# Up projection by seven block products in its own stage, with the down projection behind it

## The chip, the cores and the metric

The kernel runs on one core of one Trainium2 chip. The metric is device time in microseconds, from runs of the whole program; the profile is one further execution of it, recorded instruction by instruction. TensorE (PE) multiplies, with its weight loads listed apart (PEld); VectorE (DVE), ScalarE (ACT) and GpSimd (POOL) do the elementwise work; SyncE (SP) and POOL issue transfers. SBUF is the on-chip memory of the operands, PSUM that of the accumulators; what is named DRAM here lies off the core.

## The reference

One layer of a decoder trunk over 512 prompt tokens and 8 x 4 sample tokens, all in float32:

```python
x += W_o [ swish(g) * GroupNorm(Retention(q_r, k_r, v_r)) ; SlidingWindowSinkGQA(q_s, k_s, v_s) ]
hn = rmsnorm(x, ffn_norm_w)
up = hn @ w_up                     # 2048 x 11264: gate half g, up half u
gp = concat([conv_buf, g]); gc = conv_b + sum(gp[:, j:j+T] * conv_w[j] for j in range(3))
x += (silu(gc) * u) @ w_down       # 5632 x 2048
```

Outputs are x for both kinds of tokens, the retention states, the key and value windows, and the last two rows of g.

## The kernel before

Tokens lie in the columns: 544 of them, as two halves u of HC = 272 (256 prompt columns and 16 sample columns each). Features lie in the 128 partitions: D = 2048 is 16 tiles, the feed-forward width 5632 is FT = 44. A float32 operand is split in two parts, `hi` (a cast to fp32r on ACT, line 149) and `lo` (the difference on DVE, line 150). A product of two split operands is three matmul passes, lo x hi, hi x lo and hi x hi: `mm3`, lines 167 to 178, first those with a low part (line 173), then the high ones (line 177). Each matmul has 128 x 128 weights, a weight load of its own and 272 moving columns; the two halves u go to two PSUM banks in turn.

`project` (line 180) makes one output tile of 128 features from 2048: 16 x 6 = 96 matmuls. Its weights come in two halves of 1024 rows (512 KB each) through `stage_half`: `wraw` (3 buffers), split into `whi` and `wlo` (3 buffers each). A_hi and A_lo (16 tiles) hold the split input, C the unsplit one.

The order of the stages is: the combined input projection with retention and attention between its projects (lines 812 to 916); the output projection (918 to 992), which for each of 16 output tiles m multiplies the attention half of the input (in B) and the retention half (in A), adds the kept input, squares for the norm (POOL sums the squares, line 978) and writes the normed tile into A (`split_hn`, lines 937 to 940); and the feed-forward (999 on). There `up_group(G)` computes two feature tiles f: project the gate tile, multiply by 1/rms, convolve along the tokens (lines 1025 to 1028), project the up tile, multiply, split into Hh and Hl. `down_group(G - 1)` then multiplies the two tiles of the group before by w_down for all 16 output tiles, 12 matmuls each, and adds each into C on DVE (line 1071). In the last group `emit_y` transposes finished tiles and stores them.

The program's text is not the order of issue: a scheduler of the framework fixes the instruction order on every engine when the program is built, by which instructions it takes to be ready, earlier ones in the text first, and sets the waits. On the chip each engine then goes through its list in order. A buffer of a pool comes free when its last reader has finished; pools that lie in the space of a closed pool wait for the tiles whose space they take.

## Time and profile before

| | |
|---|---|
| median of 3 runs | 2409.63 us (2408.25 to 2410.67) |
| span of the profiled execution | 2409.4 us |
| PE busy | 2390.8 us, 99% |
| PEld busy | 2348.2 us, 97% |
| DVE busy | 1205.1 us, 50% |
| ACT busy | 651.7 us, 27% |
| DMA | 225.85 MB, 94 GB/s |

Of the profiled execution only the span is recorded, which lies 0.2 us under the median of the runs. The page of the profile gives the busy time of each engine, and groups instructions by line. A busy PE is not one at its peak, since matmuls overlap one another; its pace is read from start to start. The chain that ended last follows the work back from the last instruction; "issue" in it is time without a recorded reason. The waits say who waited for whom. The windows give busy times in stretches of the span.

### The profile page before, as it was taken

The page shows a single profiled execution, that of the slowest core. Times are in us where ns is not written, and L with a number is a line of the kernel's source. Part 1 is how long each engine was busy: PE and PEld are TensorE (multiplying, and loading weights), DVE is VectorE, ACT ScalarE, POOL GpSimd, SP SyncE. Part 2 cuts the span into 40 slices and gives each one's busy share as a digit, 9 for nine tenths or more (in the row PEclk, how much of TensorE's full clock was granted, in tenths as well). Part 3 has the DMA queues.
Part 4 walks back from the last instruction along what each step waited for, and adds up shares of the span by engine and source line. Part 5 has one row for each costly group of instructions (what it writes and reads, how often), then busy time and mean ns, then how long its engine had stood idle before and what let it go on. Part 6 is the DMA issues. An engine that isn't in the chain of part 4 may idle for free.

```text
span 2409.4 us, 43062 instructions
## 1 busy us (share of the span) xinstructions
PE 2390.8 (99%) x18743; PEld 2348.2 (97%) x18743; DVE 1205.1 (50%) x2033; ACT 651.7 (27%) x974; POOL 69.9 (3%) x240
## 2 busy tenths in 40 slices
PE   8999999999999999999999999999999999999999
PEld 7999999999999999999999999999999999999998
DVE  5545467765432544455444555444555444555444
ACT  5121235555222322222222222222222222222223
POOL 1000000000011000000000000000000000000000
PEclk8999999999999999999999999999999999999999
DMA  8333342223444332222332332323333323223223
GB/s 273 103 85 97 77 89 67 73 71 93 113 110 106 88 88 88 88 88 88 88 88 88 88 88 88 88 86 90 87 88 89 87 86 88 87 89 89 88 85 106
DMA packets 360269, 225.85 MB, mean 94 GB/s; under 512 B 41937, under 2 KB 331793, under 8 KB 360081
## 3 DMA queue, kind: packets, MB, share of 16 engines
q1 hardware_dynamic: 358576, 217.70, 32.0%
q0 software_dynamic: 1504, 5.41, 0.6%
q8 instruction: 147, 2.41, 0.4%
q14 instruction: 42, 0.34, 0.0%
HBM read 205.48 MB, written 12.86 MB: 91 GB/s over the span
## 4 chain that ended last, share of the span: by engine, by line
PE 97%; DMA 1%; SPq 1%; issue 1%; ACT 0%; DVE 0%; ACTq 0%
PE acc L173 60%; PE acc L177 30%; PE sm L719 1%; PE sm L718 1%; DMA raw<-in_w_o_dram 1%; PE sm L680 1%; PE sm L697 1%; SPq L231 0%; DMA raw<-in_w_in_dram 0%; PE sm L528 0%; PE sm L526 0%; PE sm L491 0%; PE sm L551 0%; PE sm L541 0%; PE sm L1050 0%
## 5 line engine op out<-in xcount | busy, mean ns | idle before, releaser
L173 PE MATMUL acc<-A_lo,whi 128*128 128x272 f32 x4160 | 869.2, 290 | 0.8 <-ACT whi L149 0.6
L173 PE MATMUL acc<-A_hi,wlo 128*128 128x272 f32 x4160 | 864.3, 289 | 0.0
L149 ACT CAST whi<-raw 128x1024 fp32r<-128x1024 f32 x364 | 381.6, 1048 | 1388.5 <-PE acc L177 1351.5
L150 DVE TENSOR_TENSOR wlo<-raw,whi 128x1024 fp32r<-128x1024 f32 x364 | 444.8, 1222 | 462.6 <-ACT whi L149 462.3
L173 PEld LDWEIGHTS acc<-A_lo,whi 128*128 128x128 f32 x4160 | 655.0, 189 | 7.3 <-issue 4.2
L173 PEld LDWEIGHTS acc<-A_hi,wlo 128*128 128x128 f32 x4160 | 652.4, 188 | 1.2
L177 PE MATMUL acc<-A_hi,whi 128*128 128x272 f32 x4160 | 571.3, 289 | 0.0
L177 PEld LDWEIGHTS acc<-A_hi,whi 128*128 128x128 f32 x4160 | 541.9, 189 | 1.2
L1071 DVE TENSOR_TENSOR C<-acc,C 128x544 f32<-128x544 f32 x352 | 250.7, 722 | 134.9 <-PE acc L177 133.1
L173 PE MATMUL acc<-Hl,whi 128*128 128x272 f32 x1408 | 292.3, 289 | 0.0
L173 PE MATMUL acc<-Hh,wlo 128*128 128x272 f32 x1408 | 291.3, 288 | 0.0
L177 PE MATMUL acc<-Hh,whi 128*128 128x272 f32 x1408 | 232.9, 287 | 0.0
L173 PEld LDWEIGHTS acc<-Hh,wlo 128*128 128x128 f32 x1408 | 220.2, 188 | 0.0
L173 PEld LDWEIGHTS acc<-Hl,whi 128*128 128x128 f32 x1408 | 219.5, 188 | 0.2
L177 PEld LDWEIGHTS acc<-Hh,whi 128*128 128x128 f32 x1408 | 198.0, 188 | 0.0
L1031 DVE TENSOR_TENSOR us<-acc,rstd_bc 128x544 f32<-128x544 f32 x44 | 31.9, 725 | 162.7 <-PE acc L177 162.7
L1017 DVE TENSOR_TENSOR gp<-acc,rstd_bc 128x512 f32<-128x512 f32 x44 | 30.4, 692 | 162.6 <-PE acc L177 162.5
L1028 ACT ACTIVATE cv<-cv,cwT 128x560 f32<-128x560 f32 x44 | 33.6, 764 | 136.5 <-DVE cv L1027 136.5
L173 PE MATMUL acc<-B_hi,wlo 128*128 128x272 f32 x256 | 53.3, 289 | 0.0
L173 PE MATMUL acc<-B_lo,whi 128*128 128x272 f32 x256 | 53.1, 288 | 0.0
L1021 POOL COPY co<-gp 128x2 f32<-128x2 f32 x44 | 8.2, 187 | 1372.2 <-DVE gp L1017 1372.2
L978 POOL TENSOR_TENSOR ssq<-ssq,sq 128x544 f32<-128x544 f32 x15 | 26.4, 1762 | 539.5 <-ACT sq L977 539.5
(375 smaller groups left out, 1355.8 us busy)
## 6 DMA issues: line engine op xcount, KB each, us to landing
raw<-in_w_up_dram SPq DMA_DIRECT2D x176, 512.0 KB
raw<-in_w_down_dram SPq DMA_DIRECT2D x88, 512.0 KB
raw<-in_w_in_dram SPq DMA_DIRECT2D x52, 512.0 KB
raw<-in_w_in_dram SPq DMA_DIRECT2D x32, 256.0 KB
raw<-in_w_o_dram SPq DMA_DIRECT2D x32, 256.0 KB
raw<-in_w_o_dram SPq DMA_DIRECT2D x16, 512.0 KB
C<-in_x_prompt_dram SPq DMA_DIRECT2D x8, 512.0 KB
xT_keep<-xk POOLq DMA_DIRECT2D x16, 256.0 KB, 6.1
```

What stands on the lines that cost most here:

```text
L149: act.copy(out=hi, in_=src)
L150: eng.tensor_tensor(out=lo, in0=src, in1=hi.bitcast(F32), op=sub)
L173: pe.matmul(acc[:, u, :HC], lhsT=w, rhs=x[:, u, :], start=(first and i == 0 and w is wh), stop=False)
L177: pe.matmul(acc[:, u, :HC], lhsT=wh, rhs=xh[:, u, :], start=False, stop=(last and i == n - 1))
L680: pe.matmul(po[:, 256 * kv:256 * kv + 256], lhsT=vS[:, n if n == 0 else n - 1 + kb, kv, :], rhs=t[:, kb, :], start=(j == 0), stop=(j == le ...
L697: pe.transpose(out=ptr[:, o:o + 128], in_=s[:, 2 * j + kv, 128 * kb:128 * kb + 128], identity=ident)
L718: pe.matmul(o, lhsT=q_, rhs=kX[kv][:, k0:k0 + 256], start=True, stop=False)
L978: pool.tensor_tensor(out=ssq, in0=ssq, in1=sq, op=add)
L1017: dve.tensor_tensor(out=gp[:, 2:514].rearrange("p (u c) -> p u c", u=2), in0=ag[:, :, 0:256], in1=rstd_bc[:, :, 0:256], op=mult)
L1028: act.activation(out=cva, in_=cva, func=AF.Silu, bias=cb[:, f:f + 1])
L1031: dve.tensor_tensor(out=us, in0=au, in1=rstd_bc, op=mult)
L1071: dve.tensor_tensor(out=C[:, m], in0=acc[:, :, :HC], in1=C[:, m], op=add)
```

## The change

The up projection becomes a stage of its own. For each f, the gate tile f and the up tile f, times two halves of the input features, times two halves of the tokens, are a 2 x 2 by 2 x 2 block product. It is computed with seven products of 1024 x 128 weight blocks and 272 token columns (24 matmuls each) in place of eight. The weight sums are formed on DVE in `up_pair`, the sums of the input blocks once, in `build_x`, in place in C. Partial sums are read out of PSUM by ACT in the middle of accumulations (bank `bx`, and one half of `zy`) and put together on DVE. The product of gate and up part goes to DRAM (`h_keep`), by POOL's queue. The down projection stands behind it in three groups of 16, 12 and 16 tiles f: `fill` loads them back and splits them, `down` accumulates a whole group in PSUM for two output tiles at a time. The output projection goes in two passes over m, first the attention half of its input, then the retention half; the sum x goes to DRAM (`x1_keep`) and comes back into Y for the down stage. C and the weight buffers move to the right side of the memory, so that the up stage's buffers (`ua`, `ub`) can take their place; `ring` takes turns between both.

```diff
-    wp = ctx.enter_context(tc.tile_pool(name="wp", bufs=3))
...
+    cp_ = cst.enter_context(tc.tile_pool(name="cp", bufs=1, side="right"))
+    wp = wst.enter_context(tc.tile_pool(name="wp", bufs=3, side="right"))
...
-    C = main.tile([128, KT, 2, HC], F32, name="C")
+    C = cp_.tile([128, KT, 2, HC], F32, name="C")
...
+    x1_keep = keep.tile([KT, 128, 2, HC], F32, name="x1_keep")
+    h_keep = keep.tile([FT, 128, 2, HC], F32, name="h_keep")
...
-        wo = wst.enter_context(tc.tile_pool(name="wo", bufs=1, reuse_waits="tile"))
+        mid = xst.enter_context(tc.tile_pool(name="mid", bufs=1, reuse_waits="tile"))
...
+        wo = bst.enter_context(tc.tile_pool(name="wo", bufs=1, reuse_waits="tile"))
...
+    def half_project(m, part, xh, xl):
+        hi, lo = stage_half(load_wo(m, part), 0)
+        acc = ps.tile([128, 2, 512], F32, name="acc", tag="acc", bufs=3)
+        for _ in mm3(acc, [(hi[:, k, :], lo[:, k, :], xh[:, k], xl[:, k]) for k in range(8)]):
...
+        return acc[:, :, :HC]
...
+        acc = half_project(m, 0, B_hi, B_lo)
...
+    bst.close()
+    xp = xst.enter_context(tc.tile_pool(name="xp", bufs=1, reuse_waits="tile"))
+    X_hi = xp.tile([128, 3, 8, HC], F32R, name="X_hi")
+    X_lo = xp.tile([128, 3, 8, HC], F32R, name="X_lo")
+    xop = {
+        "b21": (A_hi[:, 0:8, 0], A_lo[:, 0:8, 0]), "t4": (A_hi[:, 0:8, 1], A_lo[:, 0:8, 1]),
+        "b22": (A_hi[:, 8:16, 0], A_lo[:, 8:16, 0]), "t3": (A_hi[:, 8:16, 1], A_lo[:, 8:16, 1]),
+        "b11": (X_hi[:, 0], X_lo[:, 0]), "t1": (X_hi[:, 1], X_lo[:, 1]), "t2": (X_hi[:, 2], X_lo[:, 2]),
...
+    def split_x(name, k, src, sign=1.0):
+        hi, lo = (t[:, k] for t in xop[name])
+        if sign == 1.0:
+            split(hi, lo, src)
+        else:
+            act.activation(out=hi, in_=src, func=AF.Copy, scale=sign)
+            dve.scalar_tensor_tensor(out=lo, in0=src, scalar=sign, in1=hi.bitcast(F32), op0=mult, op1=sub)
...
+    def build_x(k):
+        a, b, c, d = C[:, k, 0], C[:, k, 1], C[:, k + 8, 0], C[:, k + 8, 1]
+        split_x("b11", k, a)
+        dve.tensor_tensor(out=b, in0=d, in1=b, op=sub)
+        split_x("t3", k, b)
+        dve.tensor_tensor(out=b, in0=b, in1=a, op=add)
+        split_x("t2", k, b, -1.0)
+        dve.tensor_tensor(out=a, in0=b, in1=d, op=sub)
+        split_x("t1", k, a)
+        split_x("b22", k, d)
+        dve.tensor_tensor(out=d, in0=b, in1=c, op=sub)
+    for i in range(KT):
+        m = i // 2 + 8 * (i % 2)
+        acc = half_project(m, 1, A_hi[:, 0:8], A_lo[:, 0:8])
+        dve.tensor_tensor(out=C[:, m], in0=acc, in1=C[:, m], op=add)
+        sth(out=x1_keep[m], in_=C[:, m])
+        if i == 0:
             act.activation(out=ssq, in_=C[:, m], func=AF.Square)
         else:
+            sq = tb1.tile([128, 2, HC], F32, name="sq2", tag="sq2", bufs=1)
             act.activation(out=sq, in_=C[:, m], func=AF.Square)
             pool.tensor_tensor(out=ssq, in0=ssq, in1=sq, op=add)
-        if m < 8:
-            split_hn(m)
-        if m == 2:
-            stT, w0, w1, w2, cb = conv_tables()
-    for m in range(8, 16):
-        split_hn(m)
-    up_ops = ((A_hi[:, 8:16], A_lo[:, 8:16]), (A_hi[:, 0:8], A_lo[:, 0:8]))
+        act.activation(out=C[:, m], in_=C[:, m], func=AF.Copy, scale=ffnw[:, m:m + 1])
+        if i % 2 == 1:
+            build_x(i // 2)
+    for k in range(8):
+        split(A_hi[:, k], A_lo[:, k], C[:, k + 8])
...
+    wst.close()
...
+    cst.close()
+    ub = ust2.enter_context(tc.tile_pool(name="ub", bufs=1, side="right", reuse_waits="tile"))
+    def ring(name, shape, dtype, n_a, n_b):
...
+    new_raw = ring("uraw", [128, 8, 128], F32, 2, 3)
+    new_sum = ring("usum", [128, 8, 128], F32, 1, 1)
+    new_hi = ring("uhi", [128, 8, 128], F32R, 2, 1)
+    new_lo = ring("ulo", [128, 8, 128], F32R, 2, 1)
+    new_g = ring("g", [128, 562], F32, 2, 0)
+    new_cv = ring("cv", [128, 562], F32, 1, 1)
+    new_tu = ring("tu", [128, 2, HC], F32, 1, 1)
+    new_us = ring("us", [128, 2, HC], F32, 1, 1)
+    new_p5 = ring("p5", [128, HC], F32, 1, 1)
...
-    ag0 = project(ps, 3, stage(cols_of(w_up[0], 0)), up_ops, between={48: rstd_ffn})
+    rstd_ffn()
...
+    def product(bank, w, x, first, last):
+        hi, lo = new_hi(), new_lo()
+        split(hi, lo, w)
+        xh, xl = xop[x]
+        for k in range(8):
+            pe.matmul(bank, lhsT=hi[:, k], rhs=xl[:, k], start=(first and k == 0), stop=False, skip_group_check=True)
+            pe.matmul(bank, lhsT=lo[:, k], rhs=xh[:, k], start=False, stop=False, skip_group_check=True)
+        for k in range(8):
+            pe.matmul(bank, lhsT=hi[:, k], rhs=xh[:, k], start=False, stop=(k == 7), skip_group_check=True)
+    def up_pair(f):
+        def load(c0, q):
+            raw = new_raw()
+            cols_of(w_up[0], c0)(raw, q)
+            return raw
+        a11, a21, a22, a12 = load(128 * f, 0), load(DFF + 128 * f, 0), load(DFF + 128 * f, 1), load(128 * f, 1)
+        bx = ps.tile([128, 512], F32, name="bx", tag="bx", bufs=2)[:, :HC]
+        zy = ps.tile([128, 2, 512], F32, name="zy", tag="zy", bufs=2)[:, :, :HC]
+        tu, us, p5 = new_tu(), new_us(), new_p5()
+        product(bx, a11, "b11", True, False)
+        act.copy(out=tu[:, 0], in_=bx)
+        s1 = new_sum()
+        dve.tensor_tensor(out=s1, in0=a21, in1=a22, op=add)
+        product(zy[:, 1], s1, "t1", True, False)
+        act.copy(out=p5, in_=zy[:, 1])
+        s2 = new_sum()
+        dve.tensor_tensor(out=s2, in0=s1, in1=a11, op=add)
+        product(bx, s2, "t2", False, False)
+        act.copy(out=tu[:, 1], in_=bx)
+        dve.tensor_tensor(out=s2, in0=s2, in1=a12, op=add)
+        product(zy[:, 1], s2, "b22", False, True)
+        dve.tensor_tensor(out=a21, in0=a21, in1=a11, op=add)
+        product(bx, a21, "t3", False, False)
+        act.copy(out=us[:, 1], in_=bx)
+        product(zy[:, 0], a12, "b21", True, True)
+        g = new_g()
...
+        dve.tensor_tensor(out=gp, in0=zy[:, :, 0:256], in1=tu[:, :, 0:256], op=add)
...
+        dve.tensor_tensor(out=gp, in0=gp, in1=rstd_bc[:, :, 0:256], op=mult)
...
+        cv = new_cv()
+        cva = cv[:, 0:560]
+        act.activation(out=cva, in_=g[:, 2:562], func=AF.Identity, scale=w2[:, f:f + 1], bias=cb[:, f:f + 1])
+        dve.scalar_tensor_tensor(out=cva, in0=g[:, 1:561], scalar=w1[:, f:f + 1], in1=cva, op0=mult, op1=add)
+        dve.scalar_tensor_tensor(out=cva, in0=g[:, 0:560], scalar=w0[:, f:f + 1], in1=cva, op0=mult, op1=add)
+        act.activation(out=cva, in_=cva, func=AF.Silu)
+        product(bx, a22, "t4", False, True)
+        act.copy(out=us[:, 0], in_=bx)
+        dve.tensor_tensor(out=us[:, 1], in0=us[:, 1], in1=p5, op=add)
+        dve.tensor_tensor(out=us, in0=us, in1=rstd_bc, op=mult)
+        dve.scalar_tensor_tensor(out=us[:, :, 0:256], in0=us[:, :, 0:256], scalar=-1.0, in1=halves_of(cv[:, 0:512]), op0=mult, op1=mult)
...
+        sth(out=h_keep[f], in_=us)
+    for f in range(FT):
+        up_pair(f)
+    ust2.close()
+    ust.close()
...
+    places = [(Xf_hi[:, i], Xf_lo[:, i]) for i in range(12)] + [(A_hi[:, i], A_lo[:, i]) for i in (*range(8, 16), *range(8))]
+    groups, at_ = [], 0
+    for n, p0 in ((16, 0), (12, 16), (16, 0)):
+        groups.append((range(at_, at_ + n), places[p0:p0 + n]))
...
+    def fill(group):
+        for f, (hi, lo) in zip(*group):
+            hs = dn.tile([128, 2, HC], F32, name="hs", tag="hs", bufs=2)
+            ld(out=hs, in_=h_keep[f])
+            split(hi, lo, hs)
...
-    def down_group(G, Hh, Hl):
-        for q in range(4):
-            raw = wraw().rearrange("p k c -> p (k c)").rearrange("p (j c) -> p j c", j=2)
-            ld(out=raw, in_=wd[256 * G:256 * G + 256, 512 * q:512 * q + 512].rearrange("(j p) c -> p j c", p=128))
-            hi, lo = (t.rearrange("p k c -> p (k c)").rearrange("p (j c) -> p j c", j=2) for t in whalf())
+    def down(group, mp, last):
+        fs, where = group
+        accs = [ps.tile([128, 2, 512], F32, name="acc", tag="acc", bufs=3) for _ in range(2)]
+        for j in range(len(fs) // 4):
+            f0 = fs[0] + 4 * j
+            raw, hi, lo = (dn.tile([128, 4, 256], d_, name=n_, tag=n_, bufs=b_) for n_, d_, b_ in (("draw", F32, 3), ("dhi", F32R, 2), ("dlo", F32R, 2)))
+            ld(out=raw, in_=wd[128 * f0:128 * f0 + 512, 256 * mp:256 * mp + 256].rearrange("(j p) c -> p j c", p=128))
             split(hi, lo, raw)
-            for i in range(4):
-                m = 4 * q + i
-                acc = ps.tile([128, 2, 512], F32, name="acc", tag="acc", bufs=3)
+            for i in range(2):
                 c = slice(128 * i, 128 * i + 128)
-                for _ in mm3(acc, [(hi[:, j, c], lo[:, j, c], Hh[:, j], Hl[:, j]) for j in range(2)]):
+                for _ in mm3(accs[i], [(hi[:, t, c], lo[:, t, c], *where[4 * j + t]) for t in range(4)], j == 0, 4 * j + 4 == len(fs)):
...
-                dve.tensor_tensor(out=C[:, m], in0=acc[:, :, :HC], in1=C[:, m], op=add)
-                if G == FT // 2 - 1 and m >= YLAG:
-                    emit_y(m - YLAG)
...
+        for i in range(2):
+            m = 2 * mp + i
+            dve.tensor_tensor(out=Y[:, m], in0=accs[i][:, :, :HC], in1=Y[:, m], op=add)
+            if last and m >= YLAG:
...
+    for m in range(KT):
+        ld(out=Y[:, m], in_=x1_keep[m])
+    fill(groups[0])
+    down(groups[0], 0, False)
+    fill(groups[1])
...
+    for mp in range(1, 8):
+        down(groups[0], mp, False)
+    fill(groups[2])
+    for mp in range(8):
+        down(groups[1], mp, False)
+    for mp in range(8):
+        down(groups[2], mp, True)
...
```

## Rows read from the trace of the kernel before

In rows of a timeline the columns are start and duration in us, engine, line, operation, output <- inputs, partitions x elements, count, and in brackets the idle time before with what ended it.

**Rows 1.** The page, parts 1 and 5: engine shares, and one group of weight loads

```profile
PE 2390.8 (99%) x18743; PEld 2348.2 (97%) x18743; DVE 1205.1 (50%) x2033; ACT 651.7 (27%) x974; POOL 69.9 (3%) x240
...
L173 PEld LDWEIGHTS acc<-A_lo,whi 128*128 128x128 f32 x4160 | 655.0, 189 | 7.3 <-issue 4.2
```

**Rows 2.** Windows: length; busy (count) by engine; clock, DMA share, GB/s

```profile
0.00:57.50 57.50, 45.91 (x317) 43.45 (x317) 29.41 (x54) 33.31 (x55) 10.98 (x25) 0.88 0.93 285
...
640.00:650.00 10.00, 8.56 (x60) 7.97 (x59) 3.81 (x6) 2.09 (x2) 0.67 (x1) 0.83 0.78 166
...
800.00:812.00 12.00, 12.00 (x95) 11.84 (x94) 10.35 (x15) 9.82 (x13) 2.98 (x5) 1.00 0.22 62
...
1036.00:1108.40 72.40, 72.40 (x579) 72.40 (x578) 35.34 (x46) 15.43 (x17) 1.17 (x8) 1.00 0.29 88
```

**Rows 3.** Chain that ended last in order of time (start, us, what), one loop period

```profile
1506.22 4.03 PE acc L173 x32
...
1578.59 4.03 PE acc L173 x32
```

**Rows 4.** Waits (waited for: us in total, times, longest): weight splits on ACT

```profile
ACT whi L149 <- PE acc L177: 1351.5, 326, 8.2
```

**Rows 5.** Timeline of PE in the attention, line 680: first pair and what follows

```profile
406.83 0.40 PE L680 MATMUL sm<-pl,vS 128*128 128x256 f32 x2
...
407.77 2.17 PE L177 MATMUL acc<-A_hi,whi 128*128 128x272 f32 x16
```

**Rows 6.** Groups by line and form on DVE: busy us, mean ns

```profile
L150 DVE TENSOR_TENSOR wlo<-raw,whi 128x1024 fp32r<-128x1024 f32 x364 | 444.8, 1222 | 462.6 <-ACT whi L149 462.3
...
L1071 DVE TENSOR_TENSOR C<-acc,C 128x544 f32<-128x544 f32 x352 | 250.7, 722 | 134.9 <-PE acc L177 133.1
...
L1027 DVE SCALAR_TENSOR_TENSOR cv<-gp,cwT,cv 128x560 f32<-128x560 f32 x44 | 35.3, 802 | 1.6
...
L1031 DVE TENSOR_TENSOR us<-acc,rstd_bc 128x544 f32<-128x544 f32 x44 | 31.9, 725 | 162.7 <-PE acc L177 162.7
L1017 DVE TENSOR_TENSOR gp<-acc,rstd_bc 128x512 f32<-128x512 f32 x44 | 30.4, 692 | 162.6 <-PE acc L177 162.5
...
L1018 DVE TENSOR_TENSOR gp<-acc,rstd_bc 128x32 f32<-128x32 f32 x44 | 8.0, 181 | 0.0
```

**Rows 7.** Groups by line and form on ACT

```profile
L149 ACT CAST whi<-raw 128x1024 fp32r<-128x1024 f32 x364 | 381.6, 1048 | 1388.5 <-PE acc L177 1351.5 <-DMA raw<-in_w_o_dram 14.0 <-DMA raw<-in_w_in_dram 11.7
...
L1028 ACT ACTIVATE cv<-cv,cwT 128x560 f32<-128x560 f32 x44 | 33.6, 764 | 136.5 <-DVE cv L1027 136.5
...
L1035 ACT CAST Hh<-us 128x544 fp32r<-128x544 f32 x44 | 28.5, 648 | 21.7 <-DVE us L1034 21.7
...
L939 ACT ACTIVATE A_hi<-C,vecT 128x544 fp32r<-128x544 f32 x16 | 11.2, 736 | 3.2 <-PE acc L177 3.2
```

**Rows 8.** Timeline of DVE inside one feature tile's gate part

```profile
1513.27 0.51 DVE L1025 TENSOR_SCALAR cv<-gp,cwT 128x560 f32<-128x560 f32 x1
1513.70 1.22 DVE L150 TENSOR_TENSOR wlo<-raw,whi 128x1024 fp32r<-128x1024 f32 x1
1514.84 0.79 DVE L1026 SCALAR_TENSOR_TENSOR cv<-gp,cwT,cv 128x560 f32<-128x560 f32 x1
```

**Rows 9.** Timelines of DVE and POOL: line 940 without and beside POOL's add

```profile
615.83 0.79 DVE L940 SCALAR_TENSOR_TENSOR A_lo<-C,vecT,A_hi 128x544 fp32r<-128x544 f32 x1
...
656.54 1.84 POOL L978 TENSOR_TENSOR ssq<-ssq,sq 128x544 f32<-128x544 f32 x1 [15.88 <-ACT sq L977]
...
657.14 1.82 DVE L940 SCALAR_TENSOR_TENSOR A_lo<-C,vecT,A_hi 128x544 fp32r<-128x544 f32 x1
```

**Rows 10.** The page, part 6: the stores issued by POOL (KB, us to landing)

```profile
xT_keep<-xk POOLq DMA_DIRECT2D x16, 256.0 KB, 6.1
```

**Rows 11.** Chain at the output projection's start: a weight load, matmuls after the hole

```profile
622.59 4.36 DMA raw<-in_w_o_dram
...
645.88 2.34 PE acc L177 x9
```

More of the change, by code (lines that the diff above doesn't have):

```diff
@@ new lines, in ring, with take @@
+    def ring(name, shape, dtype, n_a, n_b):
+        turn_ = [0]
+        def take():
+            i = turn_[0] % (n_a + n_b)
+            turn_[0] += 1
+            p, n = (ua, n_a) if i < n_a else (ub, n_b)
+            return p.tile(shape, dtype, name=name, tag=name, bufs=n)
+        return take
+    new_raw = ring("uraw", [128, 8, 128], F32, 2, 3)
+    new_sum = ring("usum", [128, 8, 128], F32, 1, 1)
+    new_hi = ring("uhi", [128, 8, 128], F32R, 2, 1)
+    new_lo = ring("ulo", [128, 8, 128], F32R, 2, 1)
@@ L987, in rstd_ffn @@
+    new_g = ring("g", [128, 562], F32, 2, 0)
[3 more added lines that the diff above has]
+    new_p5 = ring("p5", [128, HC], F32, 1, 1)
     def rstd_ffn():
-        pm = [small2(ps), small2(ps)]
-        vb = wo.tile([128, 2, HC], F32, name="vb")
-        tb = wo.tile([128, 2, HC], F32, name="tb")
+        vb, tb = new_us(), new_tu()
         for u in range(2):
-            pe.matmul(pm[u][:, :HC], lhsT=onesD, rhs=ssq[:, u, :], start=True, stop=True)
-            dve.tensor_scalar(out=vb[:, u, :], in0=pm[u][:, :HC], scalar1=EPS, scalar2=None, op0=add)
+            pm = small2(ps)
+            pe.matmul(pm[:, :HC], lhsT=onesD, rhs=ssq[:, u, :], start=True, stop=True)
+            dve.tensor_scalar(out=vb[:, u, :], in0=pm[:, :HC], scalar1=EPS, scalar2=None, op0=add)
@@ new lines, in trunk_kernel @@
+    for f in range(FT):
+        up_pair(f)
+    ust2.close()
+    ust.close()
+    upst.close()
+    dst_ = ExitStack()
+    ps = dst_.enter_context(tc.tile_pool(name="ps4", bufs=2, space=PSUM, reuse_waits="tile"))
+    yc = dst_.enter_context(tc.tile_pool(name="yc", bufs=1, side="right", reuse_waits="tile"))
+    dn = dst_.enter_context(tc.tile_pool(name="dn", bufs=1, reuse_waits="tile"))
+    Y = yc.tile([128, KT, 2, HC], F32, name="Y")
+    wd = w_down[0]
+    Xf_hi, Xf_lo = (t.rearrange("p a k c -> p (a k c)").rearrange("p (f u c) -> p f u c", u=2, c=HC) for t in (X_hi, X_lo))
@@ new lines, in trunk_kernel @@
+    fill(groups[1])
+    for q in range(3):
+        n = min(8, 18 - 8 * q)
+        cob = dn.tile([FT, 8, 128], F32, name="cob", tag="yp", bufs=2)
+        for h in range(0, n, 4):
+            w = min(4, n - h)
+            pt = small2(ps)
+            for i in range(w):
+                pe.transpose(out=pt[:FT, 128 * i:128 * i + 128], in_=co[:, 8 * q + h + i, :], identity=ident)
+            act.copy(out=cob[:, h:h + w, :], in_=pt[:FT, 0:128 * w].rearrange("p (i c) -> p i c", i=w))
+        for i in range(n):
+            r = 8 * q + i
+            dst = cp_out[0, 0, r] if r < 2 else cs_out[0, (r - 2) // 2, (r - 2) % 2]
+            st(out=dst.rearrange("(k p) -> k p", p=128), in_=cob[:, i, :])
```

128 lines of the change are left out of this document (49 added, 79 removed).

## The prediction

> **What bounds the kernel now.** I read the engine shares first. TensorE (PE) is busy 99% of the span, its weight loads 97%, VectorE (DVE) 50%, ScalarE (ACT) 27% [rows 1]; there is one weight load for every matmul, 18743 of each. A busy PE need not be a PE at its pace, so the second view is the chain of work that ended last: it runs through PE's matmuls almost without a break, and one period of the feed-forward loop (two feature tiles up, one group down: 2 x 192 + 16 x 12 = 576 matmuls) takes 1578.59 - 1506.22 = 72.37 us [rows 3], which is **125.6 ns a matmul** of 272 columns. The third view is the waits: ACT's split of weights waits 1351.5 us for PE to give a buffer back [rows 4]. So the feeders are ahead and PE's count of matmuls sets the time from 812 us on; a window of one period shows PE busy throughout, DVE 35.34 of 72.40 us, at full clock [rows 2]. The one hole near the change lies at the start of the output projection (640 to 650 us: PE 8.56 of 10 us, granted clock 0.83) [rows 2].
>
> **The change part by part.**
>
> **Matmuls removed.** Before, a pair of feature tiles (gate f and up f) costs 2 x 96 = 192 matmuls; after, seven products of 24 are 168. 44 x 24 = 1056 matmuls go: 1056 x 125.6 ns = **132.6 us**. All are on the path. Output projection (1536) and down projection (4224) keep their counts. The new products send consecutive matmuls into one PSUM bank, each with another stationary tile, where before two banks alternate. The nearest row for that is the attention's line 680: 256 columns, four matmuls in a row to one accumulator, the weights changing each time; eight of them take 406.83 to 407.77 us, 117.5 ns each [rows 5], which at that rate per column makes 124.8 ns for 272. So the new form should cost nothing extra; I keep 125.6, and let 0.8 ns x 7392 = 6 us count for the low end. *TensorE: Matmul & The Clock Gate* of the Trainium skill (section on the back-to-back issue gap) gives N/2.4 + 2.5 ns, which for 272 is 115.8 ns; no row here shows that pace, and by it the removal would be worth 122.3 us.
>
> **What the up stage adds to DVE and ACT.** DVE for one pair: seven low parts at 1.222 = 8.55; four weight sums, same shape, two SBUF inputs, 1.22 each = 4.89; the gate's adds and multiplies 2 x (0.692 + 0.181) = 1.75; two convolution steps at 0.80 = 1.60; for the up half, a 272-column add (between 0.181 for 32 and 0.692 for 512, so 0.44), 0.725, about 0.74 and 0.18 = 2.09 [rows 6]. Sum **18.9 us** of the pair's 168 x 0.1256 = **21.1 us** of PE: 89%, against 35.34/72.40 = 49% before. ACT: seven high parts at 1.048 = 7.34, five copies of 272 columns (under the 0.648 of 544; say 0.40) = 2.0, two passes of 560 columns at 0.764 = 1.5: 10.9 us, 52% [rows 7]. So by work alone both stay under PE. What can still stall PE is the order. A product lasts 24 x 0.1256 = 3.01 us and there are three pairs of split buffers, so a buffer freed at the end of one product is needed 2 x 3.01 = 6.03 us later, and needs 1.05 + 1.22 = 2.27 us; the spare is 3.76 us. (Before, a half lasts 6.03 us and the spare is 9.8.) On DVE the gate's part (1.75) and convolution (1.60) together are 3.35 us and hide; with one weight sum in front (1.22) they make 4.57 and PE waits 0.8 us. I price the order at 0.4 us a pair, the middle between 0 (work spread evenly, as in the interleaved rows of DVE before, where a split sits between two convolution steps [rows 8]) and 0.8 (one such coincidence each pair): 44 x 0.4 = **18 us**; 1.5 us a pair (two coincidences), 66 us, is the far end.
>
> What POOL does can lengthen DVE: the same line-940 instruction takes 0.79 us with POOL idle and 1.82 while POOL's 1.84 us add runs [rows 9]. *SBUF — State Buffer* of the Trainium skill (Who interferes with whom) states the rule, and it speaks against this change: a DVE instruction with two SBUF inputs contends with a GpSimd one that reads SBUF, and nearly all added DVE work has two. The trace agrees (1.82 against 0.79). In the up stage POOL's reads are three short copies, so the rule moves DVE from 89% a little up, not the sum.
>
> **Output projection in two passes.** Same matmuls, halves of 6 us instead of projects of 12. The first pass adds nothing. In the second every m costs DVE 1.22 + 0.72 and, for each two m's, a build of four adds and five low parts of 272 columns (9 x 0.44 = 4.0): 3.9 us of 6.03 per m, up to 1 more where POOL's add runs beside. Covered, by PE. Sixteen stores of x1 go on POOL's queue; nothing queued behind them but short adds. The stall of the convolution tables stays (they again take two of three raw buffers). Price 0, ends -3 and +5 (that stall gone or doubled).
>
> **From output projection to up stage.** Before, the first up product starts here without a gap (PE 12.00 of 12 us at 800 to 812 [rows 2]). After, PE has no other work. Behind the last matmul: add 0.72; store of x1 by POOL, whose end the in-place scaling of C must await (6.1 us for the like store of xT_keep [rows 10]); scaling 0.74 [rows 7]; build of the last tile, three dependent adds with their splits, about 3.5; the last split of C into A, 0.65 + 0.72; then the ring buffers that lie in C's place come free and a weight block is loaded, 0.4 + 4.4 (a w_o half lands 4.36 us after issue [rows 11]); sum 1.22, high part 1.05. Together 19.8 us, of which the first product (3.0, its operands being ready) is covered: 16.8, and about 1.2 us for slow matmuls afterwards (nine at 260 ns, the 1.2 GHz level, behind the hole at 645 us [rows 11]): **18 us**. Low end 7 (buffers not in the way: only 0.72 + 6.1 + 0.74 + 2.6, less 3.0); high end 24 (one more load in series).
>
> **From up stage to down stage.** The down products need h back from DRAM: each tile is loaded into one of two buffers (278 KB; between 2.4 us, the 4.36 us of a 512 KB load by bytes, and 4.36), cast 0.65 on ACT and subtracted 0.72 on DVE, with 0.4 of issue: 4.2 to 6.1 us for two tiles. Group 0 has 16 tiles: 33 to 49 us, against 24.1 us of PE work in the first down pass (192 matmuls). So 9 to 25 us too long, less the lead that the buffers' places allow, plus up to 9 us if a place is the last pair's us (stored first, 6.1), plus part of 16 loads of Y (4.5 MB, about 15 us at the 285 GB/s of the start window [rows 2]). I take **22 us**, ends 8 and 40. Later groups fill behind 170 us of matmuls: 0. DVE's additions into the result fall from 352 to 48: off the path, 0. Tail: the same transposes and copies, 0 (ends -2, +2).
>
> **Sum**: 2409.4 - 132.6 + 18 + 18 + 22 = 2334.8 on the profiled execution's span; the median of the runs, 2409.63, lies 0.2 above it: **2335 us**.
>
> **The rivals.**
> (a) *Seams and order hidden*: 2409.6 - 132.6 + 7 + 8 = 2292, and 2286 with 124.8 ns. For it: ACT waits on PE nearly everywhere [rows 4]. Against: the 6.1 us store and the two-buffer fill are plain chains.
> (b) *Slower: the split waits behind the gate's evacuation.* If, on ACT and DVE, the split of the pair's last product is queued behind the gate chain that waits for the product before it, PE stands for 1.75 + 0.76 + 1.60 + 0.76 + 1.05 + 1.22 = 7.1 us every pair: 2317 (the sum without a price for the order) + 312 = 2629, or 2449 at 3 us. It decides from (132.6 - 40)/44 = **2.1 us a pair**. For it: in the program's text the last split stands behind the gate's chain, cover is down from 9.8 to 3.8 us, and DVE is at 89%. Against: the order on an engine is not the program's, a split of the up weights sits inside the gate's chain [rows 8].
> (c) *Between*: order costs 1.0 to 2.0 us a pair: 2360 to 2405.
> (d) *The change doesn't do what it says*: one weight load per matmul not hidden when tiles change each time (189 ns [rows 1] instead of 125.6: 7392 x 63 ns = 466 us more than the forecast, 2801). The attention speaks against it: weights change there too [rows 5].
>
> **How the numbers follow.** Forecast 0.62 (2300 to 2375), (a) 0.16, (c) 0.10, (b) and (d) 0.10, within 5 us of before 0.02. A measurement tells about 0.2%, 5 us. Faster: 0.62 + 0.16 + 0.10 = 0.88; same 0.02; slower 0.10. The range 2285 to 2400 takes in most of (a) and (c); it leaves some 0.05 below and 0.13 above.
>
> **What would show it.** PE's matmul count 1056 lower; in the up stage a pair period near 21.5 us with DVE at 85 to 90%; between pairs no wait of PE on ACT or DVE over 1 us; one PE hole of some 15 us at the output-projection seam whose releaser is a load or a store's end; a stretch of 35 to 50 us behind the up stage in which PE waits for the h tiles; the down stage solid at 125.6 ns. Wrong if the pair period is over 23.2 us, or the seams together over 60 us.

## The result and the profile after

The changed kernel takes **2352.36 us** (2350.58 to 2352.96), the kernel before beside it 2409.64 (2408.25 to 2410.67): ratio 0.9765, 95% interval 0.9751 to 0.9778. That is 57.3 us less, where the forecast said 74.6 less: the right sign, inside the range, 17 us too good. The profiled execution's span is 2350.1 us, 59.3 under that of before.

From the page of the changed kernel, the busy time of the engines, and the chain that ended last by engine (rows of before: [rows 1]):

```profile
PE 2281.9 (97%) x17687; PEld 2224.1 (95%) x17687; DVE 1402.2 (60%) x2205; ACT 894.0 (38%) x1418; POOL 203.8 (9%) x300
...
PE 60%; DVE 20%; DMA 8%; issue 7%; ACT 4%; SPq 1%; DVEq 0%; ACTq 0%
```

17687 matmuls are 1056 fewer, as counted. PE's idle time rose from 18.6 us (2409.4 - 2390.8) to 68.2, and the chain now leaves PE for 40% of its length. To see where, I cut the trace at three lines: the last sum of the output projection (L1020), ScalarE's copy of a pair's last product (L1133, once a pair), and the sum into Y (L1201). Each row of the view by line ends with the first and the last start:

```profile
L1020 DVE TENSOR_TENSOR C<-acc,C x16: 715/723/726, 705.4 to 796.4; 128x544 f32<-128x544 f32 x16
L1133 ACT COPY us<-bx x44: 361/364/385, 839.6 to 1770.3; 128x272 f32<-128x272 f32 x44
L1201 DVE TENSOR_TENSOR Y<-acc,Y x48: 717/724/725, 1829.0 to 2341.8; 128x544 f32<-128x544 f32 x48
```

So: **seam 1 and pair 0** 839.6 - 796.4 = 43.2 us, of which 168 matmuls at 125.6 ns are 21.1: 22 lost. **Pairs 1 to 43** 930.7 us, 21.64 a pair where matmuls alone make 21.1 (907.3 in 43): 23 lost. **Seam 2 and down stage** 571.5 us for 4224 matmuls (530.5): 41 lost. In the kernel before, the same stretch runs from the last matmuls of the output projection to the last sum into C (rows of its PE and DVE timelines):

```profile
797.72 2.18 PE L177 MATMUL acc<-A_hi,whi 128*128 128x272 f32 x16
...
2402.66 0.73 DVE L1071 TENSOR_TENSOR C<-acc,C 128x544 f32<-128x544 f32 x1 [1.33 <-PE acc L177]
```

2402.7 - 799.7 (where the next matmul starts) = 1603 us for 8448 + 4224 matmuls, 1591.6 at 125.6 ns: 11 lost. The output projection itself went from 198.5 us (601.2 to 799.7) to 194.7 (600.9 to 795.6). Together -132.6 + 22 + 23 + 41 - 11 - 4 = -62, against -59.3 measured between the spans; the tail behind the last sum (8.3 us for 6.7) and the edges of the stretches are the rest. These three stretches are what the experiments are read by, since what lies ahead of them moves by several us from one kernel's execution to another's (the first sum L1020 stands between 700.2 and 709.2).

One edge has to be known. L1133 is ScalarE's copy, not the product's end. Behind the last pair the two lie 0.04 us apart, but ScalarE can be late: by 0.9 us in pair 0 of the changed kernel (0.03 to 1.8 in the other runs), which shifts that much between the first two stretches.

Where pair 0 waits, from the chain that ended last (start, length, what):

```profile
797.38 2.34 DMA x_keep<-C
...
801.02 1.28 ACT L193
...
803.30 1.28 ACT L194
...
810.55 4.13 DMA uraw<-in_w_up_dram
...
814.77 1.24 DVE usum L1102
```

PE's own waits there end by POOL's last sum of squares, by ScalarE and by VectorE:

```profile
799.60 2.18 PE L1068 MATMUL sm<-ssq,early 128*128 128x272 f32 x4 [3.82 <-POOL ssq L1027]
806.24 0.60 PE L1085 MATMUL bx<-X_lo,uhi 128*128 128x272 f32 x1 [4.46 <-ACT uhi L150]
809.94 0.60 PE L1086 MATMUL bx<-X_hi,ulo 128*128 128x272 f32 x1 [3.11 <-DVE ulo L151]
```

The store of x1 lands in 2.34 us, not the 6.1 of [rows 10]. Two table loads of 1.28 us (unlabelled lines of ACT) and Ln and Exp stand in ScalarE's queue ahead of its first split of an up weight, and a22's block is loaded only when the last reader of C is done, because its buffer lies in C's place. The windows (length, then busy of PE, PEld, DVE, ACT, POOL with counts, the granted clock, DMA share) show the clock behind the hole:

```profile
800.00:810.00 10.00, 2.43 (x6) 1.12 (x5) 8.45 (x18) 7.43 (x11) 0.84 (x3) 0.50 0.38 105
810.00:820.00 10.00, 6.61 (x31) 6.09 (x32) 5.72 (x6) 2.48 (x3) 0.00 (x0) 0.67 0.60 157
820.00:830.00 10.00, 10.00 (x70) 10.00 (x70) 5.47 (x5) 3.89 (x6) 0.00 (x0) 0.84 0.29 84
```

107 matmuls keep PE busy for 19.0 us where full pace makes 13.4: some 5 us of the 22 are matmuls at the 1.2 GHz level.

One period of the up stage, in the chain:

```profile
1279.46 1.24 DVE ulo L151
...
1280.72 4.10 DMA uraw<-in_w_up_dram
...
1284.91 0.10 DVE usum L1102
...
1297.51 1.15 DVE usum L1109
...
1298.74 1.05 ACT uhi L150
...
1301.05 1.24 DVE ulo L151
...
1302.30 4.08 DMA uraw<-in_w_up_dram
```

It closes on itself in 21.6 us without PE: VectorE's split of a21 frees a raw buffer, the next pair's a22 is loaded into it, the sum a21 + a22 waits for that load, and the rest of VectorE's queue stands behind the sum. The waits between 839 and 1771 us (total, times, longest) agree: VectorE waits for raw blocks for 127 us, while PE's own waits, all on VectorE's splits, are 13.3 us and none is longer than 0.6.

```profile
DVE usum L1102 <- DMA uraw<-in_w_up_dram: 127.0, 42, 4.5
PE zy L1086 <- DVE ulo L151: 11.8, 35, 0.6
```

At seam 2, SyncE's queue, the first down matmul, and the chain:

```profile
1773.24 9.44 SPq L1206 DMA_DIRECT2D Y<-x_keep  x16
1783.11 0.95 SPq L1164 DMA_DIRECT2D hs<-h_keep  x2
...
1792.01 1.28 PE L174 MATMUL acc<-X_lo,dhi 128*128 128x272 f32 x4 [17.54 <-ACT dhi L150]
```

```profile
1783.74 5.64 DMA hs<-h_keep
1789.40 0.66 ACT X_hi L150
1790.08 0.74 DVE X_lo L151
1790.84 3.18 DMA hs<-h_keep
...
1821.61 4.08 DMA hs<-h_keep
```

The 16 loads of Y go ahead of the first h tile (9.4 us in the queue), and then eight rounds of two tiles follow one another, load, split, next load, until 1827. The windows (columns as above, the last one GB/s) show two things more:

```profile
1780.00:1790.00 10.00, 0.00 (x0) 0.00 (x0) 0.62 (x1) 1.24 (x2) 0.00 (x0) 0.50 1.06 389
1790.00:1800.00 10.00, 7.99 (x48) 7.69 (x48) 4.53 (x6) 3.75 (x6) 0.00 (x0) 0.70 0.85 278
```

The transfers are busy throughout while Y comes in: its 4.5 MB at 389 GB/s are some 11.5 us, not far from the 9.4 us in the queue. No run tells apart which of the two the first h tile waits for. And the first matmuls behind the hole run at the 1.2 GHz level again: the 89 between 1790 and 1810 keep PE busy for 15.2 us where full pace makes 11.2.

### The profile page after: what moved, and what is told of

Read it like the earlier page. It is cut to its first block, busy times and chain, and to the rows that moved or that the text cites. A ratio compares the mean times of both kernels' runs of the same rounds, so it can differ in the third digit from the quotient of the medians.

```text
span 2350.1 us, 41993 instructions
## 1 busy us (share of the span) xinstructions
PE 2281.9 (97%) x17687; PEld 2224.1 (95%) x17687; DVE 1402.2 (60%) x2205; ACT 894.0 (38%) x1418; POOL 203.8 (9%) x300
## 4 chain that ended last, share of the span: by engine, by line
PE 60%; DVE 20%; DMA 8%; issue 7%; ACT 4%; SPq 1%; DVEq 0%; ACTq 0%
PE acc L174 32%; PE acc L178 16%; DVE ulo L151 8%; DMA uraw<-in_w_up_dram 6%; ACT uhi L150 3%; DVE usum L1109 2%; DVE usum L1106 2%; DVE cv L1130 1%; DVE cv L1129 1%; PE zy L1086 1%; DVE g L1122 1%; DVE g L1120 1%; PE zy L1088 1%; DMA hs<-h_keep 1%; PE bx L1085 1%
## 5 line engine op out<-in xcount | busy, mean ns | idle before, releaser
L174 PE MATMUL acc<-A_lo,whi 128*128 128x272 f32 x1344 | 285.9, 294 | 0.2 <-DVE A_lo L290 0.2
L174 PE MATMUL acc<-A_hi,wlo 128*128 128x272 f32 x1344 | 281.1, 290 | 0.0
L151 DVE TENSOR_TENSOR ulo<-uraw,uhi 128x1024 fp32r<-128x1024 f32 x176 | 215.0, 1222 | 7.6 <-ACT uhi L150 6.8
L150 ACT CAST uhi<-uraw 128x1024 fp32r<-128x1024 f32 x176 | 185.3, 1053 | 88.1 <-PE zy L1088 88.1
L174 PEld LDWEIGHTS acc<-A_lo,whi 128*128 128x128 f32 x1344 | 211.7, 189 | 6.4 <-issue 4.2
L174 PEld LDWEIGHTS acc<-A_hi,wlo 128*128 128x128 f32 x1344 | 212.0, 189 | 1.2
L150 ACT CAST whi<-raw 128x1024 fp32r<-128x1024 f32 x100 | 104.8, 1048 | 276.3 <-PE acc L178 233.4
L178 PE MATMUL acc<-A_hi,whi 128*128 128x272 f32 x1344 | 188.6, 292 | 0.0
L178 PEld LDWEIGHTS acc<-A_hi,whi 128*128 128x128 f32 x1344 | 177.9, 191 | 1.2
L151 DVE TENSOR_TENSOR wlo<-raw,whi 128x1024 fp32r<-128x1024 f32 x100 | 122.1, 1221 | 53.5 <-ACT whi L150 53.2
```

What stands on the lines that cost most here:

```text
L150: act.copy(out=hi, in_=src)
L151: eng.tensor_tensor(out=lo, in0=src, in1=hi.bitcast(F32), op=sub)
L174: pe.matmul(acc[:, u, :HC], lhsT=w, rhs=x[:, u, :], start=(first and i == 0 and w is wh), stop=False)
L178: pe.matmul(acc[:, u, :HC], lhsT=wh, rhs=xh[:, u, :], start=False, stop=(last and i == n - 1))
```

## The experiments

Two theories for each stretch: A says that a wait found above sets it, B that something else does and the wait is only cover. Each kernel is timed against the kernel before in five rounds; the three stretches come from its profiled execution.

| kernel | us | ratio (95%) | pair 0 | pairs 1-43 | down |
|---|---|---|---|---|---|
| changed | 2352.4 | 0.9765 (0.9751-0.9778) | 43.2 | 930.7 | 571.5 |
| e1 six raw buffers | 2328.5 | 0.9668 (0.9655-0.9682) | 42.9 | 907.3 | 570.5 |
| e2 four raw buffers | 2348.4 | 0.9750 (0.9736-0.9765) | 44.2 | 928.8 | 571.6 |
| e3 Y behind the fill | 2349.5 | 0.9756 (0.9742-0.9769) | 42.4 | 923.7 | 574.5 |
| e4 rstd late | 2346.9 | 0.9733 (0.9714-0.9753) | 41.0 | 925.0 | 570.8 |
| e5 fill through four buffers | 2347.2 | 0.9738 (0.9722-0.9753) | 43.4 | 931.2 | 566.4 |
| e7 rstd late, a22 left | 2342.8 | 0.9723 (0.9707-0.9739) | 35.6 | 928.1 | 572.6 |
| e8 fill within last pair (*) | 2349.6 | 0.9754 (0.9739-0.9770) | 43.2 | 937.9 | 563.5 |
| e9 e8 and Y out (*) | 2340.6 | 0.9724 (0.9709-0.9738) | 43.2 | 939.8 | 553.1 |
| e10 Y out | 2347.5 | 0.9748 (0.9735-0.9762) | 43.5 | 932.1 | 562.1 |
| best1 (*) | 2320.2 | 0.9626 (0.9608-0.9644) | 34.7 | 911.8 | 564.3 |
| best2 (*) | 2313.1 | 0.9604 (0.9591-0.9618) | 35.3 | 914.3 | 556.4 |
| best3 | 2305.0 | 0.9582 (0.9569-0.9596) | 34.5 | 907.7 | 553.8 |

With five raw buffers and an up stage of unchanged text the pairs took 924 to 932 us; why they vary is not settled. A difference below 8 us in that column, and what it does to a total, is not used.

(*) In these four runs the fill of the first h tiles stands in ScalarE's queue ahead of the last product's copy, which comes 5.3, 5.7, 2.5 and 2.1 us behind the product's end, so the copy is no fair edge. From the end of the product the last two columns are 933.4 and 568.8 (e8), 934.9 and 558.8 (e9), 909.4 and 566.8 (best1), 912.1 and 558.6 (best2), beside 931.6 and 571.5 in the changed kernel.

### The raw blocks

```diff
-    new_raw = ring("uraw", [128, 8, 128], F32, 2, 3)
+    new_raw = ring("uraw", [128, 8, 128], F32, 2, 4)
```

> The ring of raw blocks of the up stage has six buffers in place of five; nothing else in the text changes. Theory A (the pair period of 21.65 us is a loop through the raw ring: the last split of a21 frees a buffer, a 4.1 us load fills it, the sum a21 + a22 waits for it, and VectorE's queue of the next pair stands behind that sum): with six buffers a22's load waits for a11's release, which is 3.6 us earlier in a pair, so the loop has slack and the period falls to TensorE's own 21.1 to 21.2 us. 43 x 0.45 to 0.54 us = 19 to 23 us less than the changed kernel's 2352.4: 2329 to 2333 us, ratio 0.967 to 0.968 to the kernel before, and VectorE's total wait for raw loads falls from 131 us to under 20. Theory B (the written order and VectorE's 18.6 us of work a pair cost the half microsecond): 2349 to 2355 us, ratio 0.975 to 0.977, period 21.6.

Measured: 2328.5 us, 43 periods of 21.10. The wait, and the window of the 43 pairs, here and (last line) in the changed kernel:

```profile
DVE usum L1102 <- DMA uraw<-in_w_up_dram: 8.2, 26, 0.7
...
839.20:1746.50 907.30, 906.92 (x7226) 906.17 (x7225) 754.59 (x899) 438.03 (x602) 129.08 (x213) 1.00 0.37 110
...
839.60:1770.30 930.70, 917.06 (x7219) 907.20 (x7218) 743.72 (x899) 428.91 (x602) 150.28 (x215) 1.00 0.36 108
```

PE is busy for all but 0.4 us, VectorE does the same 899 instructions, and nothing is lost. The size and the place are A's; VectorE's work as the cause, the one half of B, is excluded, its order, the other half, is taken up next. The other way, with four buffers (`2, 2`):

> The ring of raw blocks has four buffers in place of five. Theory A (loop through the raw ring): a22's load now waits for a22's own split of the pair before, 6.6 us later in a pair than the split of a21; the loop is then 18.6 us of VectorE work from the sum to the splits of a21 and a12, 1.2 us of a22's split and 4.2 us of load, 24.0 us, less what of the gate's arithmetic is put into the wait: period 22.3 to 24.1 us, 2380 to 2460 us, ratio 0.988 to 1.02. Theory B (order and VectorE's work): period 21.6 us as with five, 2350 to 2356 us, ratio 0.975 to 0.978.

Measured: 2348.4 us, 21.60 a pair: no slower, so A's size for this run was wrong, and B's period came. VectorE's rows over part of one period:

```profile
1275.55 2.46 DVE L151 TENSOR_TENSOR ulo<-uraw,uhi 128x1024 fp32r<-128x1024 f32 x2
1279.87 1.23 DVE L151 TENSOR_TENSOR ulo<-uraw,uhi 128x1024 fp32r<-128x1024 f32 x1 [1.86 <-ACT uhi L150]
1283.31 1.23 DVE L1102 TENSOR_TENSOR usum<-uraw 128x1024 f32<-128x1024 f32 x1 [2.22 <-DMA uraw<-in_w_up_dram]
```

The order on the engine is not the same: the split of a22 now stands ahead of the next pair's sum (in the changed kernel behind it), and the sum waits 90.3 us in all. And the load that the sum waits for is issued at 1278.03, when the second of the two splits of 1275.55 ends (a12's, by TensorE's order of the products), not behind a22's own split, which ends at 1281.1: the step that A counted on isn't in this run, and the loop from the sum over the splits to the load is about as long as with five. The scheduler, which fixes the order at build time, wrote another list for another ring. So the ring's depth doesn't set the period by itself. My reading, that what costs is a sum standing in VectorE's queue in front of ready work while its block is on the way, fits the three runs but isn't tested by itself. With six buffers the list changed too, so the ring and the order are not told apart; that the wait and the loss vanish together (127 us and 23, 8 us and 0) is shown.

### Seam 1

```diff
-    rstd_ffn()
...
         product(bx, s2, "t2", False, False)
+        if f == 0:
+            rstd_ffn()
```

> The norm's rstd (two matmuls, Ln, Exp and VectorE's refinement) is written in pair 0 behind the third product in place of ahead of pair 0, so that ScalarE splits a11 before it loads the two tables. Theory A (the two table loads and Ln and Exp, 4.5 us on ScalarE, hold the first product back): the first product starts 3 to 4.5 us earlier and the first pair ends 2 to 4 us earlier: 2348 to 2350.5 us, ratio 0.9747 to 0.9757. Theory B (a22's load into the place of C, which starts only when the last reader of C is done, holds the first pair, so what is ahead of it is hidden): the first product starts earlier but the first pair ends within 1 us of where it did: 2351 to 2353 us, ratio 0.976 to 0.977.

Measured: pair 0 ends 41.0 us behind the last sum, 2.2 earlier, as A said. The total fell by 5.5 us, more than A said; in the profiled execution the pairs took 5.7 us less, which this edit doesn't explain. Then also a22 of pair 0 away from C's place (`uraw` 3 and 2, `g` 0 and 2):

> The rstd is written late in pair 0 as in the run with rstd late, and the raw ring is split three to two so that a22 of pair 0 lies left and not in the place of C (the two buffers of g change sides for it); five raw buffers as before. Theory A (a22's load into the place of C holds the first pair): the first pair ends 37 to 39 us behind the last sum of the output projection (43.2 in the changed kernel, 41.0 with rstd late alone). Theory B (the second buffer of the sums and the third of the splits lie in the place of C as well, so the last reader of C holds the pair anyway): 40 to 42 us. Both: the period of the later pairs stays at 21.5 to 21.65; 2342 to 2346 us by A, 2346 to 2350 us by B.

Measured: 35.6 us, 7.6 less than the changed kernel, more than A's 4 to 6. The chain there: the first block's load is issued when POOL's last sum of squares is done, and the first product runs without a break from 808.1 (9.7 us behind the start of the last sum, 13.5 in the changed kernel). Behind it TensorE waits 1.3 us for the next, 3.4 in the changed kernel.

```profile
801.57 4.10 DMA uraw<-in_w_up_dram
805.74 1.05 ACT uhi L150
...
808.10 0.59 PE bx L1084
```

Of the 22 us lost, about 2 were the table loads and 5 the block in C's place; the other 13 or more stay in every run here.

### Seam 2

The Y loads written behind the fill in the text:

> The 16 loads of Y are issued behind the 16 loads of the first fill in place of ahead of them. Theory A (the Y loads stand 9.4 us in the queue and some 11 us on the transfers ahead of the first h tile): the first h tile lands 8 to 11 us earlier, and the first pass of the down projection ends by as much earlier: 2341 to 2345 us, ratio 0.9715 to 0.973. Theory B (the fill itself, 16 tiles through two buffers at 2.4 us a tile, sets the seam, and the Y loads only take turns with it): 2349 to 2353 us, ratio 0.975 to 0.9765.

Measured: the down stage took 574.5 us, 3 more. The scheduler put the loads of Y between those of h all the same (SyncE's queue):

```profile
1774.47 1.07 SPq L1164 DMA_DIRECT2D hs<-h_keep  x2
1775.59 1.37 SPq L1207 DMA_DIRECT2D Y<-x_keep  x3
```

So this run moved the loads without taking them out of the way, and decides nothing about them; A's gain did not come, and that the total is B's doesn't show B. The fill through four buffers:

```diff
+            if group is groups[0] and f % 2:
+                hs = dn.tile([128, 4, 256], F32, name="yp", tag="yp", bufs=2).rearrange("p c d -> p (c d)")[:, 0:2 * HC].rearrange("p (u c) -> p u c", u=2)
+            else:
+                hs = dn.tile([128, 2, HC], F32, name="hs", tag="hs", bufs=2)
```

> The first fill of the down projection takes its 16 h tiles through four buffers in place of two (every second tile uses a buffer of the output stage, which is idle then); the 16 loads of Y stay ahead of them. Theory A (the seam is a serial chain of load, ScalarE copy, VectorE subtraction and the next load, eight rounds of two tiles at 5.3 us): four rounds of some 6 us, and the first pass ends 10 to 13 us earlier after the last up product (58.7 us in the changed kernel, 46 to 49 here): 2339 to 2343 us, ratio 0.971 to 0.9725. Theory B (the transfers bind: 16 Y tiles and 16 h tiles at about 390 GB/s): the seam stays within 4 us of 58.7: 2348 to 2353 us, ratio 0.9745 to 0.9765.

Measured: 566.4 us, 5.1 less: between the two. The first sum into Y came 48 us behind the last up product in place of 59, as A said, but the stage gained only half of that. The first sum is a poor mark: ahead of it TensorE had done 206 of the down matmuls and all 18 small ones of `co` (the rows of g for an output) in the changed kernel, and 180 and 8 here (PE's windows by line). The 26 make 3.3 us and the 10 small ones 1.3; TensorE's only later wait is 0.7 us. So these are the 5.3 us between the two gains, and almost nothing is lost in the later passes. The fill moved into the last pair:

```diff
         product(bx, a22, "t4", False, True)
+        if f == FT - 1:
+            early_fill(0, 16)
```

(`early_fill` loads and splits tiles 0 to 15 through the raw ring; `fill(groups[0])` goes.)

> The 16 h tiles of the first group are loaded and split within the last pair of the up stage, through the ring of raw blocks, into the places that the last pair's products give free (12 behind the third product, 4 behind the fifth). Theory A (the fill is what the seam costs): from the last up product to the first sum of the down projection 58.7 us in the changed kernel becomes 30 to 38: 24.1 us of matmuls and the first w_down block's load and split; 2324 to 2332 us, ratio 0.9645 to 0.968. Theory B (the Y loads ahead of the first w_down block on the queue, and the place of the stage's own buffers, hold the start anyway): the first matmul starts no earlier than 10 us before the one of the changed kernel: 46 to 50 us, 2340 to 2345 us.

Measured: 2349.6 us: A fell (the first sum comes 45.1 us behind the copy, not 30 to 38), and the total lies above B's too. The 8 us by which the down stage looks shorter are mostly the edge: the last product ends at 1770.0, and its copy stands behind splits of the fill in ScalarE's queue. From the product's end the stage is 2.7 us shorter. The rest of the last pair's elementwise work is late too (VectorE ends it at 1779.3, 9.3 us behind the product; 2.8 in the changed kernel). The Y loads start when it is done, and the first w_down block stands behind them in the queue:

```profile
1768.83 1.15 PE L1088 MATMUL bx<-A_hi,uhi 128*128 128x272 f32 x8
1775.25 0.38 ACT L1144 COPY us<-bx 128x272 f32<-128x272 f32 x1
1779.39 9.40 SPq L1215 DMA_DIRECT2D Y<-x_keep  x16
1789.25 1.74 SPq L1202 DMA_DIRECT2D draw<-in_w_down_dram  x3
...
1796.79 1.28 PE L174 MATMUL acc<-X_lo,dhi 128*128 128x272 f32 x4 [16.78 <-ACT dhi L150]
```

TensorE starts its first down matmul 26.8 us behind the end of the last up product, 21.7 in the changed kernel: what the fill saves behind the last pair it mostly costs there. With Y taken out of the seam, where no order of the text can bring it back:

```diff
+            if group is groups[0]:
+                act.copy(out=Y[:, m], in_=accs[i][:, :, :HC])
...
+            if group is groups[1]:
+                x1 = dn.tile([128, 2, HC], F32, name="hs", tag="hs", bufs=2)
+                ld(out=x1, in_=x1_keep[m])
+                dve.tensor_tensor(out=Y[:, m], in0=Y[:, m], in1=x1, op=add)
```

> As the run with the fill within the last pair, and the 16 loads of Y leave the seam as well: the first group's sums are copied from PSUM to Y, and x1 is loaded tile by tile during the second group and added there (16 more VectorE adds of 0.72 us). Theory A (with the fill gone, the 16 Y loads ahead of the first w_down block are what the seam waits for): TensorE starts 11 to 13 us earlier behind the last up product than with the fill alone (20.6 us there), and the down stage, from the last up product's copy to the last sum of Y, falls from 563.5 us to 550 to 553: 2336 to 2340 us, ratio 0.9695 to 0.9715. Theory B (the two buffers of w_down's splits and the second group's fill hold it anyway): 558 to 564 us, 2344 to 2350 us.

> The changed kernel with the 16 Y loads taken out of the seam alone (x1 is added in the second group); the first fill stays behind the up stage, through two buffers. Theory A (the Y loads and the serial fill stand one behind the other): the first h tile lands some 9.5 us earlier and the whole chain with it, down stage 571.5 us in the changed kernel, 560 to 564 here: 2341 to 2345 us, ratio 0.9715 to 0.9735. Theory B (only the serial fill counts, as the run with Y behind the fill said): 569 to 572 us, 2349 to 2353 us.

Measured: down stage from the copy 562.1 us with Y out alone, 553.1 with both, as A said of each (the second at its edge). From the product's end, neither, fill, Y, both: 571.5, 568.8, 562.1, 558.8. Y is worth 9.4 and 10.0 whether the fill is there or not, so it stands in the way by itself; the fill within the last pair is worth 2.7 and 3.3. In the run with both, TensorE's first matmul:

```profile
1787.03 1.28 PE L174 MATMUL acc<-X_lo,dhi 128*128 128x272 f32 x4 [7.10 <-ACT dhi L150]
```

It starts 9.1 us earlier behind the last product than with the fill alone (9.5 behind the copy), not the 11 to 13 of A. The totals missed A's ranges by 1 and 2.5 us, without a cause that I can show; the intervals of the ratios reach into A's (0.9709 and 0.9735 are their lower ends).

### Together

> Together: six raw buffers (three on either side), rstd late, and the first h tiles filled within the last pair. If the parts add up: 20 to 24 us for the ring, 2 to 5 for the first seam, 20 to 28 for the second: 2295 to 2310 us, ratio 0.9525 to 0.959. If only the ring and the first seam do: 2324 to 2330 us, ratio 0.9645 to 0.967.

Measured: 2320.2 us, between the two ranges: seam 1 and the ring about as in the single runs (34.7 us, and 909.4 for 43 pairs from product's end to product's end), of seam 2 only 4.7 us from the product's end (7.2 from the copy), since the fill in the pair delays the copy here too, by 2.5 us.

> Six raw buffers, rstd late, the first fill within the last pair, Y out of the seam, and the loads of h tiles and x1 and the 18 small stores on GpSimd's queue, so that SyncE's holds only the w_down blocks. Theory A (in the down stage's start the w_down blocks wait in SyncE's queue behind loads that wait for a buffer): the down stage falls from 564.3 us in the combination before to 540 to 550: 2296 to 2308 us, ratio 0.953 to 0.958. Theory B (only Y's 12 us count): 550 to 553 us, 2308 to 2310.

Measured: 2313.1 us, above both, with the down stage at 556.4. GpSimd's queue gave the w_down blocks a free way: in the stage's first 70 us they wait for their own buffers alone (59.3 us) but for 1.4. The loads of h and x1 on it landed in 2.7 to 5.0 us (median 3.1), and TensorE waits for none of them: its waits in the whole stage are 12.0 us, the longest 4.8 for the first w_down split. Why A's gain didn't come is open.

> Six raw buffers (three on either side), rstd late, Y out of the seam (x1 added in the second group) and the first fill behind the up stage through four buffers; nothing of the fill lies within the last pair. If the stages add up as in the single runs: the first pair ends 35 to 36 us behind the last sum of the output projection (43.2 in the changed kernel), the 43 periods after it take 907 us (930.7), and from there to the last sum of Y 555 to 559 us (571.5); 43 to 48 us less than the changed kernel: 2304 to 2310 us, ratio 0.9565 to 0.959. If the four buffers gain nothing once Y is gone, 562 us in the last stage and 2310 to 2314.

Measured: **2305.0 us**, ratio 0.9582 (0.9569 to 0.9596), 101 us under the kernel before beside it (2406.1), and 44 under the changed kernel by the two ratios (47 by the medians of the two series). Its three stretches:

```profile
L1020 DVE TENSOR_TENSOR C<-acc,C x16: 715/724/725, 706.0 to 796.9; 128x544 f32<-128x544 f32 x16
L1133 ACT COPY us<-bx x44: 386/386/391, 831.4 to 1739.1; 128x272 f32<-128x272 f32 x44
...
L1207 DVE TENSOR_TENSOR Y<-acc,Y x32: 714/725/725, 1963.0 to 2292.9; 128x544 f32<-128x544 f32 x32
```

34.5, 907.7 and 553.8 us: 49.4 less (8.7, 23.0, 17.7), and the span of the profiled execution is 48.9 less. The single runs gave 7.6, 23.4, and 9.4 + 5.1; so the parts add up, the last by 3 us better than their sum.

## Why the forecast was right in sign and 17 us too good

**Matmuls removed**: right. 1056 fewer, and with the raw wait gone the new form runs at 907.3 / (43 x 168) = 125.6 ns, the price taken from [rows 3]; one accumulator bank with changing tiles costs nothing, as [rows 5] said. The formula that I cited from *TensorE: Matmul & The Clock Gate* of the Trainium skill (the section on the back-to-back issue gap) gives 115.8 ns; the section states it for an isolated matmul and says that in a stream of weight loads and matmuls both set the spacing. The stream here ran at 125.6, and the measurement decides.

**Order in the up stage**: 18 us forecast, 23 measured, by another mechanism. I priced coincidences of the gate's arithmetic with the splits; the run with six buffers has all of that arithmetic, in another order, and loses nothing. The step that failed is the list of buffers: I counted the spare of the split buffers (3.76 us) and not that of the raw ones, whose late load holds VectorE for 127 us. That 18 lies near 23 is luck. VectorE's load was also put too high: 743.7 us busy of 930.7, 80%, not 85 to 90; its full-size instructions last 1.22 us but follow one another every 1.14 (1286.06, 1287.19, 1288.33), which a sum of durations misses. Rival (b), the last split behind the gate's chain, didn't come.

**Output projection in two passes**: the stall of the convolution tables, which I said stays, went (PE is busy all of 640 to 650 us, 8.56 of 10 before); 198.5 became 194.7 us, 0.8 us beyond the low end of -3.

**Seam 1**: 18 forecast, 22 measured, by terms that were wrong both ways (the terms listed make 19.5 us, not 19.8, which changes nothing). The store of x1 took 2.34 us of the 6.1 I had from [rows 10]; against that I had left out the two table loads with Ln and Exp in front of the first split (2.2 us by e4), and I priced the slow matmuls at 1.2 us where the windows show some 5. The load into C's place I had in the sum, and it is there (4.13 us). I expected one hole that a load or store ends; there were several, ended by POOL's sum, ACT and DVE.

**Seam 2**: 22 forecast, 41 measured, 30 if the 11 that the kernel before loses in its feed-forward are taken off; this is the term that was mis-sized most, and just past its upper end of 40. The fill's rounds were right (5.4 us for two tiles, of 4.2 to 6.1). The Y loads were in my list, but I took a value below the sum of the parts, as if they ran beside the fill; they stand ahead of the h tiles, and the runs without Y show that their 9.4 to 10.0 us come on top, whatever the fill does. Slow matmuls behind this hole had no term at all; they are some 4 us. By the mark that I had set (both seams together under 60 us) the forecast failed: 63. And the raw wait, with a period of 21.64 us, stayed under the mark for the period (23.2), which therefore couldn't show it.

**What is left of 17**: on the profiled executions the forecast of 2334.8 is 15.3 us short. Seam 2 gave 19 more than forecast, order 5, seam 1 4, the tail 2; against that the output projection gave 4, and the 11 us that the kernel before loses in its feed-forward, which the forecast carried along, are gone from the account. The remaining 2 us: wherever a run has both, its time lies some 2 us above its span (2352.16 and 2350.1 here), and the forecast went from span to time with 0.2. So misses of both signs partly cancel, and the total came out nearer than its terms.

## What to carry to other kernels

When a stage is rebuilt, list every ring of buffers with the time from a buffer's last reader to its next need, the raw loads' too: one that was short showed as a wait of an engine that is not the bound, and as small losses on the one that is. At a seam, write down the order of each queue, and add what stands one behind the other. Taking away one of two serial costs brings its own part only if the work doesn't land where it delays something else; moving a load in the program's text need not take it out of the way when a scheduler writes the order. And choose an edge between stretches that the edit doesn't move: the end of a product, not a copy that waits in another engine's queue.
